# Summing the key exponents of the HGRN levels by two identity products on TensorE

## The chip, the cores and the metric

The kernel runs on one core of one Trainium2 chip. The metric is the device time of one execution, in microseconds (us). The engines have their profile names: PE is TensorE (PEld its weight loads), DVE is VectorE, ACT is ScalarE, POOL is GpSimd and SP is SyncE, which here only issues transfers.

## What is computed

Two layers of a hybrid block over 2048 latent tokens and 256 context tokens, with a model width of 1024. In each layer one input projection feeds four groups of heads: differential attention, a bidirectional gated linear recurrence (HGRN2), windowed attention and an mLSTM. Their outputs are gated, pass one output projection and are added to the stream. The change lies in the recurrence, of which this is the core:

```
cum = jnp.cumsum(log_f, axis=3)
...
diff = cum[:, :, :, :, None, :] - cum[:, :, :, None, :, :]
decay = jnp.exp(jnp.where(tri[:, :, None], diff, -jnp.inf))
a = jnp.einsum('bhnlk,bhnsk,bhnlsk->bhnls', q, k, decay)
o = (jnp.einsum('bhnls,bhnsv->bhnlv', a, v)
     + jnp.einsum('bhnlk,bhnkv->bhnlv', q * jnp.exp(cum), s_start))
```

The matrix `a` needs, for each pair of positions, the product of a query and a key under a decay that depends on both.

## The kernel before

Tokens are worked on in tiles of 128; for HGRN a group is two tiles. Within a tile the kernel builds `a` by halving: at a level m (64, 32, 16, 8, 4, 2, 1) blocks of 2m positions are cut in two halves, and the decay between the halves is split at their border into one factor on the keys and one on the queries. `prepare(li)` makes both factors for a level. The key exponent is a sum of `lk` (log of the key less its cumulated gate) and `cm` (the cumulated gate) at the border; the query exponent is a difference of two places in `cm`. Both lie in the tile `E` (128 partitions, two halves of 512 columns, float32): `E[:, 0]` for keys and `E[:, 1]` for queries. One exponential is taken over both, `QQ` is the query times `E[:, 1]`, and 16 small products (`gA`, 64x64) with the keys give the level's part of `a`, which DVE or ACT puts into `Ad` or `Am`. An eighth step (m = 0, the diagonal) adds whole tiles and is not touched by the change. There are 9 groups in the first layer and 8 in the second, so 17 x 7 = 119 levels.

The HGRN stream runs at the end of each layer, woven together with three others: windowed attention (`ss`, `spv`, with the transposed probabilities `swt`), the mLSTM (`mqk`, `mnum`) and the output stream (`ft` transposes, `fx` the output projection, `xt` the result). Here this is called the woven stretch. `weave` picks the next piece of a stream by due times that are counted in PE time: the helper `mm` (line 94 is its matmul) adds each product's columns, four times as many for float32, to `pe_ns`. `prepare` runs two levels ahead of the products that use it. A scheduler of the language then sets each engine's order from its own model of the times; an engine works through its queue in that order. PSUM tiles of these streams come from `bank`, which hands out four banks in turn under the tag "gp". `lk` and `cm` are loaded from DRAM for each group by the SP queue (line 1463), two buffers deep.

The helpers are one line each, so many operations share a line in the profile: `tt` is line 108, `act` line 105, `mm` line 94 and `tp` line 101.

Of the kernel before, what the change touches and what calls it, by code (L numbers as in the profile page):

```python
# [14 lines left out]
AF = mybir.ActivationFunctionType  # L15
ALU = mybir.AluOpType
# [17 lines left out]
P = 128  # L34
# [25 lines left out]
def view(ap, off, *dims):  # L60

    return bass.AP(ap.tensor, ap.offset + off, [list(ap.ap[0])] + [list(d_) for d_ in dims])
# [11 lines left out]
def kernel(  # L74
# [8 lines left out]
    V, A, G, PE, SP = nc.vector, nc.scalar, nc.gpsimd, nc.tensor, nc.sync  # L83
# [9 lines left out]
    def mm(o, lhsT, rhs, start, stop):  # L93
        PE.matmul(o, lhsT=lhsT, rhs=rhs, start=start, stop=stop)  # L94
        n = 1
        for d_ in rhs.shape[1:]:
            n *= d_
        pe_ns[0] += max(128, n * 4 if rhs.dtype == F32 else n) / 2.4
# [5 lines left out]
    def act(o, i, f, **kw):  # L104
        A.activation(out=o, in_=i, func=f, **kw)  # L105

    def tt(e, o, a, b, op):
        return e.tensor_tensor(out=o, in0=a, in1=b, op=op)  # L108
# [5 lines left out]
    ident = const.tile([P, P], F32, tag="ident", name="ident")  # L114
# [144 lines left out]
    for l in range(n_layers):  # L259
# [941 lines left out]
        with ExitStack() as st4:  # L1201
# [11 lines left out]
            def bank(shape, name):  # L1213
                turn_[0] += 1
                if gps2 and turn_[0] % GPB == 0:
                    return gps2.tile(shape, F32, tag="gp", name=name)
                return gps.tile(shape, F32, tag="gp", name=name, bufs=GPB - 1)
# [226 lines left out]
            def hgrn_stream():  # L1444
# [10 lines left out]
                for g in range(ngrp):  # L1455
# [3 lines left out]
                    def ld(src, tag):  # L1459

                        a = hg.tile([P, 2, 512], F32, tag=tag, name=tag)
                        for d in range(2):
                            SP.dma_start(a[:, d].rearrange("p (b t) -> p b t", b=2),
                                         src[d, :, :, cols].rearrange("b p t -> p b t"))
                        return a
# [4 lines left out]
                    lk, cm = ld(dhk, "lk"), ld(dhc, "cm")  # L1470
# [8 lines left out]
                    def prepare(li):  # L1479

                        m = lv[li]
                        E = hg.tile([P, 2, 512], F32, tag="E", name="E", bufs=EB)
                        if not m:
                            tt(G, E, lk, cm, ALU.add)
                            act(E, E, AF.Exp)
                            tt(G, E[:, 0], E[:, 0], E[:, 1], ALU.add)
                            ops[li] = E[:, 0], q
                            return
                        QQ = hg.tile([P, 512], F32, tag="QQ", name="QQ", bufs=2)


                        n_ = (2 * m, 256 // m)
                        halves = ((m, 2), n_, (1, m))
                        tt(G, view(E[:, 0], 0, *halves), view(lk, 0, (512 + m, 2), n_, (1, m)),
                           view(cm, m - 1, (513, 2), n_, (0, m)), ALU.add)
                        tt(G, view(E[:, 1], 0, *halves), view(cm, 512, (m - 512, 2), n_, (1, m)),
                           view(cm, 512 + m, (-513, 2), n_, (0, m)), ALU.subtract)
                        act(E, E, AF.Exp)
                        tt(V, QQ, q, E[:, 1], ALU.mult)
                        KK = E[:, 0]  # L1500
                        ops[li] = KK, QQ

                    prepare(0)
                    prepare(1)
                    qe = hg.tile([P, 2, 512], F32, tag="qe", name="qe")
                    act(qe, cm, AF.Exp)
                    tt(G, qe, qe, bc(q, 1, 2), ALU.mult)
                    yield 2 * g, HGL, None
                    for li in range(len(lv)):
                        KK, QQ = ops.pop(li)  # L1510
                        pss = [bank([P, 4, 64], "gA") for _ in range(2)]
                        for n in range(4):
                            o = (n % 2) * 256 + n // 2 * P
                            for pa_ in range(2):
                                r_ = slice(pa_ * 64, pa_ * 64 + 64)
                                for a in range(2):
                                    k0, q0 = o + a * 64, o + (a if li else 1 - a) * 64
                                    mm(pss[pa_][a * 64:a * 64 + 64, n], KK[r_, k0:k0 + 64], QQ[r_, q0:q0 + 64],
                                       True, True)
                        for pa_, ps in enumerate(pss):  # L1520
                            if li > 1:
                                V.copy_predicated(Ad[pa_], bc(hgm[:, li], 1, 4), ps)
                            elif li:
                                A.copy(Ad[pa_], ps)
                            else:
                                amv = Am[pa_].rearrange("p i a q -> p (i a) q")
                                for a in range(2):
                                    h_, o_ = slice(a * 64, a * 64 + 64), slice((1 - a) * 64, (1 - a) * 64 + 64)
                                    A.copy(amv[h_, :, o_], ps[h_])
                        if li + 2 < len(lv):  # L1530
                            prepare(li + 2)
                        yield 2 * g + HSTEP * (li + 1), HGW, None
# [201 lines left out]
```

## Time and profile before

| | |
|---|---|
| median of three runs | 4094.21 us (4089.32 to 4104.06) |
| the profiled execution | 4102.18 us, its span 4100.4 us |
| first woven stretch (layer 1) | about 1540 to 2170 us |
| second woven stretch (layer 2) | about 3570 to 4100 us |
| granted TensorE clock, mean | 0.913 of full speed |

Times within the span are counted from its start. The woven stretches are the only places in which the changed lines run; together they are some 1,150 us of the span. In a row of the trace a float32 product shows as two matmul records, and a weight load goes with each; records of one line that follow closely are merged into one row, whose length is that from the first start to the last end.

### The profile page before, as it was taken

The page shows a single profiled execution, that of the slowest core. Times are in us where ns is not written, and L with a number is a line of the kernel's source. Part 1 is how long each engine was busy: PE and PEld are TensorE (multiplying, and loading weights), DVE is VectorE, ACT ScalarE, POOL GpSimd, SP SyncE. Part 2 cuts the span into 40 slices and gives each one's busy share as a digit, 9 for nine tenths or more (in the row PEclk, how much of TensorE's full clock was granted, in tenths as well). Part 3 has the DMA queues.
Part 4 walks back from the last instruction along what each step waited for, and adds up shares of the span by engine and source line. Part 5 has one row for each costly group of instructions (what it writes and reads, how often), then busy time and mean ns, then how long its engine had stood idle before and what let it go on. Part 6 is the DMA issues. An engine that isn't in the chain of part 4 may idle for free. (4 is left out here: it accounts for less than half of the span.)

```text
span 4100.4 us, 77666 instructions
## 1 busy us (share of the span) xinstructions
PE 3358.2 (82%) x29798; PEld 2269.8 (55%) x29798; DVE 2831.4 (69%) x4343; ACT 2330.9 (57%) x4662; POOL 2375.0 (58%) x1701
## 2 busy tenths in 40 slices
PE   6988878888768996888888988778887698758888
PEld 4656645444546765555557466444445476545554
DVE  5158888888896647465544398988888865467665
ACT  4245655556655636566654266656666665456764
POOL 4443455443445538798966535665334564488885
PEclk8999989999989995898889999999998899869999
DMA  6356866667656628577845457667676584366783
GB/s 211 91 149 150 186 136 159 140 141 154 145 128 157 161 95 200 149 194 185 205 119 177 126 125 151 135 140 155 148 162 142 125 193 116 106 162 170 183 194 104
DMA packets 1267259, 622.12 MB, mean 152 GB/s; under 512 B 931972, under 2 KB 1214152, under 8 KB 1266888
## 3 DMA queue, kind: packets, MB, share of 16 engines
q1 hardware_dynamic: 1164520, 490.65, 53.1%
q10 hardware_dynamic: 102368, 126.52, 9.2%
q8 instruction: 234, 3.83, 0.4%
q14 instruction: 137, 1.12, 0.1%
HBM read 291.76 MB, written 131.23 MB: 103 GB/s over the span
## 5 line engine op out<-in xcount | busy, mean ns | idle before, releaser
L108 POOL TENSOR_TENSOR p<-p,p 128x1024 f16<-128x1024 f32 (+2 forms) x264 | 629.4, 2385 | 792.7 <-ACT p L1084 722.8
L105 ACT ACTIVATE p<-scr,sm 128x1024 f32<-128x1024 f32 (+2 forms) x528 | 628.3, 1194 | 417.8 <-DVE sm L1073 145.2
L94 PE MATMUL ptm<-wb,hh 128*128 128x256 f16 (+2 forms) x5024 | 835.6, 273 | 32.6 <-DVE dSs L111 7.9
L1048 DVE TENSOR_REDUCE sm<-scr 128x1 f32<-128x1024 f32 (+2 forms) x528 | 699.3, 1327 | 218.3 <-PE scr L94 214.5
L94 PE MATMUL pfm<-hh,wb 128*128 128x512 f16 (+1 forms) x2592 | 805.7, 375 | 32.7 <-DVE gz L111 10.1
L94 PE MATMUL ptm<-wb,hl 128*128 128x256 f16 (+2 forms) x2512 | 672.1, 273 | 1.7 <-POOL hl L108 1.7
L94 PEld LDWEIGHTS <-wb 128*128 128x128 f16 x3888 | 378.1, 101 | 414.3 <-issue 84.0
L94 PE MATMUL scr<-Ks,Qs 128*128 128x512 f16 (+1 forms) x1296 | 364.8, 381 | 284.5 <-ACT p L105 279.4
L94 PEld LDWEIGHTS <-hh 128*128 128x128 f16 x5024 | 480.1, 100 | 133.9 <-issue 40.0
L94 PE MATMUL pfm<-hl,wb 128*128 128x512 f16 (+1 forms) x1296 | 485.6, 375 | 0.0
L111 DVE SCALAR_TENSOR_TENSOR p<-p,sm,p 128x1024 f32<-128x1024 f32 (+2 forms) x264 | 413.8, 1568 | 8.1
L94 PEld LDWEIGHTS <-Qs 128*128 128x128 f16 x1296 | 130.7, 102 | 425.2 <-issue 354.5
L94 PE MATMUL fx<-wo,mh 128*128 128x512 f16 x1088 | 342.4, 396 | 16.8 <-DVE xt L111 8.5
L1084 ACT CAST p<-p 128x1024 f16<-128x1024 f32 (+2 forms) x264 | 297.7, 1128 | 39.2 <-DVE p L111 33.8
L94 PEld LDWEIGHTS <-wt 128*128 128x128 f16 x4640 | 243.9, 102 | 71.4 <-DMA wt<-p 24.4
L94 PE MATMUL pv<-Vs,wt 128*128 128x128 f16 (+1 forms) x4640 | 258.5, 213 | 21.9 <-DMA wt<-p 13.5
L94 PEld LDWEIGHTS <-hl 128*128 128x128 f16 x2512 | 250.8, 100 | 35.4 <-POOL hl L108 3.4
L108 POOL TENSOR_TENSOR ph<-swp,ph 128x640 f16<-128x640 f32 (+2 forms) x136 | 196.0, 1442 | 53.7 <-ACT ph L1335 44.3
L108 POOL TENSOR_TENSOR E<-lk,cm 128x512 f32<-128x512 f32 (+1 forms) x136 | 204.8, 1506 | 34.6 <-DMA cm<-dhc 17.8
L94 PE MATMUL fx<-wo,mlo 128*128 128x512 f16 x544 | 212.9, 391 | 1.4 <-DVE mlo L108 1.1
L105 ACT ACTIVATE E<-E 128x1024 f32<-128x1024 f32 x136 | 143.2, 1054 | 102.8 <-POOL E L108 98.9
L108 DVE TENSOR_TENSOR QQ<-hq,E 128x512 f32<-128x512 f32 x119 | 143.8, 1214 | 65.2 <-ACT E L105 46.7
(301 smaller groups left out, 6577.2 us busy)
## 6 DMA issues: line engine op xcount, KB each, us to landing
wraw<-in_w_in_dram SPq DMA_DIRECT2D x60, 512.0 KB
dgt<-ga ACTq DMA_DIRECT2D x68, 256.0 KB
r1b<-dr SPq DMA_DIRECT2D x68, 256.0 KB
gtt<-dgt SPq DMA_DIRECT2D x34, 512.0 KB
mraw<-in_w_mod_dram SPq DMA_DIRECT2D x64, 256.0 KB
vi<-dhi SPq DMA_DIRECT2D x49, 256.0 KB
KSb<-dsk SPq DMA_DIRECT2D x56, 192.0 KB
Ks<-dka SPq DMA_DIRECT2D x64, 144.0 KB
```

The costliest lines, as they stand in the source:

```text
L94: PE.matmul(o, lhsT=lhsT, rhs=rhs, start=start, stop=stop)
L105: A.activation(out=o, in_=i, func=f, **kw)
L108: return e.tensor_tensor(out=o, in0=a, in1=b, op=op)
L111: V.scalar_tensor_tensor(out=o, in0=a, scalar=s, in1=b, op0=op0, op1=op1)
L1048: V.tensor_reduce(sm[:, m * 2 + j:m * 2 + j + 1], ps[:, :n], AX.X, ALU.min)
L1084: A.copy(wl[:, :n], p[:, :n])
```

## The change

The sum of the key exponents leaves POOL. A new PSUM tile `e0` (128x512, from `bank`) receives two products with the identity matrix as the stationary operand, the first of `lk`, the second of `cm` accumulated onto it, both read and written through the same strided views as before. ACT takes the exponential from `e0` into `E[:, 0]`, and in a second instruction that of `E[:, 1]`. The difference for the queries stays on POOL.

```diff
-                        tt(G, view(E[:, 0], 0, *halves), view(lk, 0, (512 + m, 2), n_, (1, m)),
-                           view(cm, m - 1, (513, 2), n_, (0, m)), ALU.add)
+                        e0 = bank([P, 512], "e0")
+                        mm(view(e0, 0, *halves), ident, view(lk, 0, (512 + m, 2), n_, (1, m)), True, False)
+                        mm(view(e0, 0, *halves), ident, view(cm, m - 1, (513, 2), n_, (0, m)), False, True)
+                        act(E[:, 0], e0, AF.Exp)
                         tt(G, view(E[:, 1], 0, *halves), view(cm, 512, (m - 512, 2), n_, (1, m)),
                            view(cm, 512 + m, (-513, 2), n_, (0, m)), ALU.subtract)
-                        act(E, E, AF.Exp)
+                        act(E[:, 1], E[:, 1], AF.Exp)
                         tt(V, QQ, q, E[:, 1], ALU.mult)
```

On PE, in the last group of the second layer, near its first levels, the order before has the level's products `gA` between the mLSTM's `mnum` and the output projection's `fx` (`wo` is its weight, `mh` the upper half of the input):

```order
L94 MATMUL mnum<-cst_35559,g0b 128x130
L94 MATMUL mnum<-v_42627,r1b 128x65 x2
L94 MATMUL gA<-QQ,E 64x64 x18
L94 LDWEIGHTS mh
L94 MATMUL fx<-wo_38415,mh 128x512
```

The order after, in the same group, where `e_44350` is the `e0` of its third level:

```order
L94 MATMUL spv<-SVc,swt 128x128
L94 LDWEIGHTS swt
L94 MATMUL spv<-SVc,swt 128x64
L94 MATMUL gA<-QQ,E 64x64 x16
L94 MATMUL e_44350<-lk,ident 128x2x16x16
L94 MATMUL e_44350<-cm,ident 128x2x16x16
L94 MATMUL mnum<-cst_35748,g0b 128x130
L94 MATMUL mnum<-v_43822,r1b 128x65 x2
```

Two products of 512 float32 columns now stand directly behind a level's `gA`, and what follows in PE's queue (`mnum` here) stands behind them.

On POOL, in the same group, the order before has both halves of a level one behind the other:

```order
L108 TENSOR_TENSOR E<-lk,cm 128x2x4x64
L108 TENSOR_TENSOR E<-cm 128x2x4x64
L108 TENSOR_TENSOR E<-lk,cm 128x2x8x32
L108 TENSOR_TENSOR E<-cm 128x2x8x32
L108 TENSOR_TENSOR ph<-swp,ph 128x640
L108 TENSOR_TENSOR yt<-yt,gtt 128x512
```

After, one instruction for each level is left, and the levels stand closer to each other:

```order
L108 TENSOR_TENSOR E<-cm 128x2x16x16
L108 TENSOR_TENSOR yt<-yt,gtt 128x512 x2
L108 TENSOR_TENSOR E<-cm 128x2x32x8
L108 TENSOR_TENSOR ph<-swp,ph 128x640
L108 TENSOR_TENSOR E<-cm 128x2x64x4
```

The first add of a level (`E<-lk,cm`) is gone from POOL's queue at all 119 places; the one for m = 0, over 1024 columns, remains.

## Rows read from the trace of the kernel before

**Rows 1.** The page: busy time, share of the span and instructions of each engine.

```profile
PE 3358.2 (82%) x29798; PEld 2269.8 (55%) x29798; DVE 2831.4 (69%) x4343; ACT 2330.9 (57%) x4662; POOL 2375.0 (58%) x1701
```

**Rows 2.** Stretches: busy time of each engine (x instructions), granted clock, DMA share, GB/s.

```profile
core 0: us, PE busy (x) PEld busy (x) DVE busy (x) ACT busy (x) POOL busy (x), PEclk, DMA share, GB/s
1540.00:1650.00 110.00, 71.32 (x735) 57.27 (x737) 83.11 (x121) 68.89 (x172) 97.72 (x77) 0.58 0.88 201
1650.00:2110.00 460.00, 392.70 (x4129) 270.61 (x4130) 261.89 (x473) 289.65 (x773) 398.21 (x317) 0.87 0.70 176
3570.00:3700.00 130.00, 77.96 (x924) 60.71 (x925) 81.68 (x125) 75.06 (x164) 108.28 (x79) 0.64 0.69 173
3700.00:4040.00 340.00, 294.87 (x3260) 194.69 (x3259) 234.88 (x395) 224.77 (x643) 305.45 (x250) 0.95 0.72 178
```

**Rows 3.** The same stretches, instructions on tile E alone (on DVE: the QQ products).

```profile
1540.00:1650.00 110.00, 14.88 (x356) 12.69 (x360) 15.63 (x11) 12.62 (x12) 32.86 (x25) 0.58 0.88 201
1650.00:2110.00 460.00, 61.62 (x1920) 49.80 (x1920) 63.76 (x52) 63.20 (x60) 160.59 (x120) 0.87 0.70 176
3570.00:3700.00 130.00, 18.00 (x512) 15.04 (x512) 17.68 (x16) 19.00 (x18) 52.08 (x38) 0.64 0.69 173
3700.00:4040.00 340.00, 46.80 (x1486) 35.47 (x1486) 46.73 (x41) 48.38 (x46) 123.70 (x91) 0.95 0.72 178
```

**Rows 4.** The page: chain that ended last, share of the span by engine, by line.

```profile
POOL 4%; PE 3%; DMA 2%; issue 1%; SPq 1%; ACT 1%; DVE 1%; ACTq 0%; POOLq 0%; DVEq 0%
POOL E L108 2%; PE fx L94 1%; POOL yt L108 1%; POOL ph L108 1%; DMA cm<-dhc 1%; PE ptm L94 0%; DMA g0b<-dg 0%; POOL r1b L108 0%; SPq L1385 0%; DMA swt<-ph 0%; PE go L94 0%; DMA gtt<-dgt 0%; POOL g0b L108 0%; SPq L1383 0%; PE gA L94 0%
```

**Rows 5.** Waits in 3575 to 4100: total us, times, longest us.

```profile
ACT E L105 <- POOL E L108: 50.9, 31, 4.5
...
PE spv L94 <- DMA swt<-ph: 29.9, 15, 4.7
...
PE gA L94 <- DVE QQ L108: 17.7, 10, 4.7
POOL E L108 <- DMA cm<-dhc: 14.6, 7, 3.3
```

**Rows 6.** POOL's first adds, 1548 to 2170 and 3575 to 4100: busy us, mean ns | idle before.

```profile
L108 POOL TENSOR_TENSOR E<-lk,cm 128x512 f32<-128x512 f32 x63 | 84.0, 1333 | 18.8 <-DMA cm<-dhc 5.6 <-PE mnum L94 5.5 <-PE gA L94 4.6
...
L108 POOL TENSOR_TENSOR E<-lk,cm 128x512 f32<-128x512 f32 x56 | 77.6, 1387 | 15.8 <-DMA cm<-dhc 12.3 <-DMA lk<-dhk 2.1 <-PE gA L94 1.4
```

**Rows 7.** PE in order of time: start us, length us, operation, records.

```profile
3741.94 0.39 PE L94 MATMUL mnum<-cst,g0b 128*128 128x130 f32 x2
3742.16 0.56 PE L94 MATMUL mnum<-v,r1b 128*128 128x65 f32 x4
...
3770.67 0.69 PE L94 MATMUL gA<-QQ,E 64*64 64x64 f32 x32
3771.29 0.60 PE L94 MATMUL fx<-wo,mh 128*128 128x512 f16 x2
3771.74 0.38 PE L94 MATMUL fx<-wo,mlo 128*128 128x512 f16 x1
```

**Rows 8.** A dense stretch of the input projections (columns as in rows 2).

```profile
1400.00:1450.00 50.00, 47.54 (x391) 34.92 (x390) 24.14 (x49) 24.18 (x47) 23.36 (x20) 1.00 0.46 125
```

**Rows 9.** ACT by shape: the exponential of E, one of 512 columns, reads of PSUM.

```profile
L105 ACT ACTIVATE E<-E 128x1024 f32<-128x1024 f32 x136 | 143.2, 1054 | 102.8 <-POOL E L108 98.9
...
L105 ACT ACTIVATE ga<-ga 128x512 f32<-128x512 f32 x68 | 42.6, 626 | 4.9 <-DVE carry L650 3.2 <-POOL fm L108 0.6
...
L105 ACT ACTIVATE swp<-ss,ssm 128x512 f32<-128x512 f32 x16 | 10.9, 678 | 21.3 <-DVE ssm L1331 18.2 <-DMA v<-dmv 3.0
...
L1550 ACT COPY O<-go 128x512 f32<-128x512 f32 x17 | 9.7, 572 | 0.5 <-PE go L94 0.5
```

**Rows 10.** The chain where a group begins: start us, us, what.

```profile
3912.60 0.47 SPq L1463
3913.11 5.27 DMA cm<-dhc
3918.45 0.18 issue
3918.65 0.19 issue
3918.84 4.20 POOL E L108 x4
```

## The prediction

> **What bounds the kernel now.** I read the page first: over the whole span PE is busy 82%, DVE 69%, POOL 58% [rows 1]. That is an average over stages, and the change touches one stage only, so the second view is that of stretches. Each woven stretch has a start-up and a steady part [rows 2]. In the steady parts (1650 to 2110 and 3700 to 4040, together 800 us) PE is busy 392.7 of 460 and 294.9 of 340 us, 85% and 87%; POOL is busy 398.2 and 305.5 us, 87% and 90%. Two engines are nearly full at once. PE stands idle 67.3 + 45.1 = 112 us there, and its clock is granted at 0.87 and 0.95 of full speed. In the start-ups (110 and 130 us) the clock is 0.58 and 0.64, near the lower of its two levels, 1.2 and 2.4 GHz; PE is busy 71.3 and 78.0 us and POOL 97.7 and 108.3 us, so POOL leads there, with DMA at a share of 0.88 in the first.
>
> The chain that ended last runs more through POOL than through any other engine (4%), and E is POOL's largest line on it, 2% [rows 4]. The waits agree: ACT's exponential waits 50.9 us for POOL's E in the second woven stretch, and PE waits 17.7 us for QQ, which follows from it [rows 5]. So there is a reason to take work from POOL. The question is what it costs where it goes, because PE is as full as POOL.
>
> **What is removed.** 119 adds on POOL, 63 of 84.0 us and 56 of 77.6 us together, 161.6 us or 1.36 us each [rows 6]. In a group of seven levels that is 9.5 us of POOL.
>
> **What is added on PE.** Two float32 products of 512 columns for each level. The trace has no such product, so I take the nearest float32 one: `mnum` of 130 columns starts at 3741.94 and the next line at 3742.16, so 0.22 us or 1.69 ns a column [rows 7]. Two `fx` of 512 half-precision columns start at 3771.29 and the next one at 3771.74, 0.22 us each, a fourth per column [rows 7]. A product of 512 float32 columns is then 512 x 1.69 ns = 0.87 us, a level 1.73 us, and 119 levels 206 us at the full clock. At the lower level of the clock it is twice that. For size: all 16 `gA` products of a level take 0.62 us (3770.67 to 3771.29) [rows 7], so PE's work for a level becomes almost four times what it was.
>
> **Where it falls.** The QQ products count the levels in each stretch: 11 and 52, 16 and 41 (one too many in all, at a border) [rows 3]. For the steady parts that is 52 x 1.73 = 90.0 us and 41 x 1.73 = 70.9 us at the full clock.
> - At the clock granted now: 392.7 + 90.0 / 0.87 = 496.1 us and 294.9 + 70.9 / 0.95 = 369.5 us, 865.6 us of PE in 800 us. Without any idle time that is 66 us more. The densest stretch that I found, in the input projections, has PE busy 47.54 of 50 us, 95.1% [rows 8]. With that share, 865.6 / 0.951 = 910 us: +110.
> - With the clock at 1.00, as it is in that dense stretch: 392.7 x 0.87 + 90.0 = 431.6 and 294.9 x 0.95 + 70.9 = 351.0, together 782.6, / 0.951 = 823 us: +23.
>
> The clock should rise, since it is lowest in the start-ups, where PE is idle most, and 1.00 in the dense stretch [rows 2, 8]; but it will not be full throughout, as PE still waits for other engines. I take the middle of 23 and 110: **+67 us**. The Trainium skill, "TensorE: Matmul & The Clock Gate", Part 1 on the clock gate, says that the throttled state is the default and that activity releases it. By that rule alone the second case would hold, +23. The trace agrees in its direction: 0.58 and 0.64 in the start-ups, 0.87 and 0.95 behind them.
>
> **Start-ups.** 11 and 16 levels cost 11 x 1.73 / 0.58 = 32.8 and 16 x 1.73 / 0.64 = 43.3 us of PE, 76 in all, and PE is idle for 38.7 and 52.0 us [rows 2, 3]. POOL, which leads there, is relieved by 27 x 1.36 = 37 us. The bounds are -37 and +76; I take 0, since the two act against each other and DMA is nearly full anyway. The cover is PE's idle time; where it doesn't fit, up to 76 us come back.
>
> **The transfer of cm.** A group begins with a load of lk and cm. In the row shown cm is issued last at 3913.11 and takes 5.27 us, with POOL starting E at 3918.84 [rows 10]. POOL waited 14.6 us for cm in the second woven stretch and 5.6 in the first [rows 5, 6], 20 in all. After the change PE waits too: the first `e0` of a group stands in its queue, and behind it stand `fx`, `ss` and `spv` of other streams. The bounds are 0 and 17 x 5.3 = 90 us. I take half of the waits that POOL has, **+10**, since PE will mostly be late itself.
>
> **ACT, bank and DVE.** One exponential of 1054 ns becomes two: 626 ns from SBUF, and from PSUM between 572 (a copy) and 678 (an exponential with a sum), so 144 to 250 ns more, 17 to 30 us over 119 levels [rows 9]. ACT is busy 63% and 66% in the steady parts [rows 2], so I count nothing; without that cover it is 30. `e0` holds one of the four banks from its first product to the end of its exponential, while a level's `gA` takes two; the trace has no row for a wait that this makes, and its bounds are with the second rival. DVE's work is the same.
>
> **Sum.** 67 + 0 + 10 = +77 us on the profiled execution's 4102.2, so 4179; the median of the runs shown is 8.0 lower, so **4171 us**. The forecast's own range is 4117 (+23, no other cost) to 4224 (+110 and the 20 us of waits for cm).
>
> **Rivals.**
> 1. *POOL sets the pace and PE has room (faster).* For it: POOL's place on the chain [rows 4] and ACT's 50.9 us of waiting [rows 5]. The gain would be the first adds' part of E on the chain: E is 2%, 82 us; all of POOL's work on E in rows 3 is 369 us, the first adds are 161.6 or 44% of it, so 36 us less: 4058. It decides if PE can take 161 to 178 us more into 112 us of idle time; even with the clock at 1.00 PE would have to be 98% busy (782.6 of 800). Against it: no stretch that I saw is so dense. Chance 0.10.
> 2. *The products do not fill idle time (much slower).* They stand behind the level's `gA`, so they wait with it, for QQ, for a bank, for cm, as `spv` does for swt (29.9 us) [rows 5], and everything else in PE's queue waits with them. Then nothing is hidden: 206 us, or the 865.6 us of above at the present 86% busy, 1007 us in place of 800. That gives 4300, with cm 4310. Chance 0.15.
> 3. *No measurable change.* The clock rises to 1.00 and the products fit with 2% idle: 800 us again, 4094. A change of 0.3%, 12 us, is about the least that a measurement of this kernel tells from none. Chance 0.06.
> 4. *Strided products are slow.* The views step through `lk`, `cm` and PSUM in pieces of m columns. If a strided product took twice the time, 206 us more would come on top: near 4377; if only m = 1 did, 17 levels x 1.73 = 29 us: 4200. No row shows a strided float32 product. The Trainium skill, "PSUM — Partial Sum Buffer", Specifications, says that any access pattern that is not contiguous slows matmuls significantly, which speaks against the change; no run so far shows it. A float32 column already takes four times a half-precision one [rows 7], which leaves time for each write. Chance 0.05.
>
> The forecast itself has 0.64. Slower is 0.64 + 0.15 + 0.05 = 0.84, the same 0.06, faster 0.10. The range 4085 to 4310 leaves out most of the first rival (0.09), half of the second (0.07) and most of the fourth (0.03).
>
> **What the changed profile would show.** `e0` rows on PE, four records a level, 1.7 us from the first start to the next line; PE busy above 92% in the steady parts and POOL below 75%; a higher granted clock; the waits of ACT for POOL's E much smaller, and in their place waits for PE. The time between the output stream's tiles grows. If `e0` rows take over 2.5 us at the full clock, rival 4 is right; if PE's idle share stays at 14% while the stretches lengthen by 200 us, rival 2; if POOL is still the fuller engine, rival 1. The prediction is wrong if the products are far cheaper than 0.87 us, or if the new order moves other streams' work apart so that a wait which I haven't seen grows.

## The result, and the profile after

The changed kernel takes 4161.05 us (median; 4157.16 to 4166.45), the kernel before in the same comparison 4094.26 us. The ratio is 1.0161, 95% interval 1.0139 to 1.0183: 67 us slower, where 77 were forecast. The profiled execution has a span of 4155.3 us against 4100.4, 55 us more: 12 less than the medians, since the one of the kernel before took 4102.18 us, more than its median, and that of the changed kernel 4157.16, less than its median.

The page's first part, against [rows 1]:

```profile
PE 3494.7 (84%) x30274; PEld 2297.4 (55%) x30274; DVE 2808.8 (68%) x4343; ACT 2336.3 (56%) x4781; POOL 2205.8 (53%) x1582
```

PE gained 476 records (four for each of 119 levels) and 136.5 us of busy time, POOL lost 119 instructions and 169 us, ACT gained 119 instructions and 5.4 us.

The stretches of the changed kernel, columns as in [rows 2]; the second steady part is cut at 4020 us here, so that experiments can be set beside it:

```profile
1540.00:1650.00 110.00, 82.93 (x799) 56.16 (x799) 75.09 (x121) 69.89 (x184) 79.67 (x63) 0.80 0.85 195
1650.00:2110.00 460.00, 438.91 (x4299) 272.13 (x4299) 257.55 (x468) 290.19 (x822) 324.88 (x262) 0.98 0.69 175
3700.00:4020.00 320.00, 294.72 (x2746) 182.87 (x2745) 171.21 (x317) 188.67 (x561) 204.85 (x174) 0.95 0.65 162
```

The same cut of the kernel before:

```profile
3700.00:4020.00 320.00, 279.94 (x3070) 184.75 (x3072) 217.70 (x366) 213.34 (x612) 285.60 (x234) 0.95 0.73 179
```

In the steady parts PE is now busy 95% and 92%, POOL 71% and 64%: one full engine in place of two. In the first the clock went from 0.87 to 0.98; in the second it was 0.95 and stayed there. The counts show what that means for the work done: in 460 us of the first steady part PE made 4299 matmul records, the products among them, against 4129 before; in 320 us of the second 2746 against 3070. By this the loss sits in the second.

The output stream says the same. First the kernel before, then the changed one: instructions on the tile `xt`, count, durations in ns, first and last start in us (the 18 POOL adds belong to the first layer's tiles, the 32 DVE sums to the second's).

```profile
L111 DVE SCALAR_TENSOR_TENSOR xt<-fx,xt x32: 676/682/694, 3676.4 to 4092.8; 128x512 f32<-128x512 f32 x32
L108 POOL TENSOR_TENSOR xt<-xt,yt x18: 2337/2357/2798, 1670.6 to 2161.1; 128x1024 f32<-128x1024 f32 x18
```

```profile
L111 DVE SCALAR_TENSOR_TENSOR xt<-fx,xt x32: 677/692/693, 3684.0 to 4147.4; 128x512 f32<-128x512 f32 x32
L108 POOL TENSOR_TENSOR xt<-xt,yt x18: 2337/2354/2394, 1661.5 to 2159.7; 128x1024 f32<-128x1024 f32 x18
```

From its first tile to its last the output stream takes 498.2 us in place of 490.5 in the first layer (+8) and 463.4 in place of 416.4 in the second (+47). The first tile comes 9 us earlier (1670.6 to 1661.5), and from the end of the first layer's stream to the first tile of the second's it is 9 us longer (1515.3 to 1524.3). Only the 47 stands clear of the scatter between traces: in E4 and E7 below, which have all the work of the kernel before and no product, the first tile comes at 1682.7 and 1661.0 us, the first layer's stream takes 474.7 and 503.3 us, and the second's 408.2 and 413.2.

The products themselves, in the changed kernel's PE rows in order of time, as in [rows 7]:

```profile
1662.10 1.02 PE L94 MATMUL e<-lk,ident 128*128 128x512 f32 x2
1662.96 1.02 PE L94 MATMUL e<-cm,ident 128*128 128x512 f32 x2
1663.82 0.33 PE L94 MATMUL go<-vi,Am 128*128 128x64 f32 x2
...
3785.86 1.17 PE L94 MATMUL e<-lk,ident 128*128 128x512 f32 x2
3786.86 1.06 PE L94 MATMUL e<-cm,ident 128*128 128x512 f32 x2
```

A level takes 1.72 us from 1662.10 to the next line at 1663.82; this is m = 64. At 3785.86, a level of m = 2, the first product alone takes 1.00 us to the second's start. The last level of the group that begins at 1662.10, m = 1, takes 1.89 us:

```profile
1693.66 1.15 PE L94 MATMUL e<-lk,ident 128*128 128x512 f32 x2
1694.65 1.06 PE L94 MATMUL e<-cm,ident 128*128 128x512 f32 x2
1695.55 0.25 PE L94 MATMUL spv<-SVb,swt 128*128 128x128 f16 x2
```

The view of the tile `e`, for the changed kernel, tells what else belongs to it (min/median/max in ns; then PE's pauses for lk and ACT's waits for the products, us and times):

```profile
L94 PE MATMUL e<-lk,ident x238: 592/612/1222, 1542.4 to 4085.5; 128*128 128x512 f32 x119
L94 PE MATMUL e<-cm,ident x238: 592/592/1061, 1547.4 to 4086.4; 128*128 128x512 f32 x119
L105 ACT ACTIVATE E<-e x119: 569/597/617, 1552.0 to 4087.1; 128x512 f32<-128x512 f32 x119
...
  DMA lk<-dhk: 4.7, 2
...
  ACT E L105: 61.0, 39
```

ACT waits 61.0 us for the products. The waits of 3575 to 4100 us answer to [rows 5] (the changed kernel's stream is not quite at its end there):

```profile
ACT E L105 <- POOL E L108: 50.1, 28, 6.8
ACT E L105 <- PE e L94: 30.4, 19, 5.7
...
POOL E L108 <- DMA cm<-dhc: 15.8, 5, 4.3
...
PE gA L94 <- ACT E L105: 13.1, 6, 3.2
...
PE spv L94 <- DMA swt<-ph: 8.0, 6, 2.2
...
PE gA L94 <- DVE QQ L108: 4.5, 2, 4.2
```

ACT waits for POOL as long as before, now for the difference that is left there, and for PE besides. PE's wait for swt has shrunk from 29.9 to 8.0 us; that of `gA` for QQ and E together is 17.6, where it was 17.7 for QQ alone. PE paused once for a transfer before work on `e`: the 4.7 us above are one pause, counted on the weight load (2.4 us) and on the product (2.2 us).

### The profile page after: what moved, and what is told of

It reads as the page before. It is cut to its first block, busy times and chain, and to the rows that moved or that the text cites. A ratio compares the mean times of both kernels' runs of the same rounds, so it can differ in the third digit from the quotient of the medians.

```text
span 4155.3 us, 78592 instructions
## 1 busy us (share of the span) xinstructions
PE 3494.7 (84%) x30274; PEld 2297.4 (55%) x30274; DVE 2808.8 (68%) x4343; ACT 2336.3 (56%) x4781; POOL 2205.8 (53%) x1582
## 5 line engine op out<-in xcount | busy, mean ns | idle before, releaser
L108 POOL TENSOR_TENSOR ph<-swp,ph 128x640 f16<-128x640 f32 (+2 forms) x136 | 186.2, 1369 | 119.5 <-ACT ph L1335 99.6
L108 POOL TENSOR_TENSOR E<-cm 128x512 f32<-128x512 f32 x119 | 147.7, 1245 | 62.7 <-DMA cm<-dhc 37.9
L94 PEld LDWEIGHTS <-mh 128*128 128x128 f16 x1088 | 103.3, 103 | 121.0 <-issue 40.6
```

## The experiments

Each kernel was compared with the kernel before in the same session; that one's medians were 4094.74 (E1 to E4), 4100.31 (E5 to E8) and 4094.41 us (E9 to E11). Differences are taken within a session, but for those between the changed kernel (beside 4094.26) and E1, E2 or E5.

**E1 to E4: which part costs, and which order.**

E1 takes both the add and the products away:

```diff
-                        e0 = bank([P, 512], "e0")
-                        mm(view(e0, 0, *halves), ident, view(lk, 0, (512 + m, 2), n_, (1, m)), True, False)
-                        mm(view(e0, 0, *halves), ident, view(cm, m - 1, (513, 2), n_, (0, m)), False, True)
-                        act(E[:, 0], e0, AF.Exp)
+                        act(view(E[:, 0], 0, *halves), view(lk, 0, (512 + m, 2), n_, (1, m)), AF.Exp, scale=1e-3)
```

> Neither the add on POOL nor the products on PE: ACT takes the exponential of the strided lk alone (scaled by 0.001, to stay finite), so the border's term is left out and the decays are not the reference's; instruction counts elsewhere are those of the changed kernel. Theory (the changed kernel is paced by PE, and its 67 us are the products' streaming time less what the clock gives back): without the products the time falls below the kernel before, 4050 to 4090 us, as POOL's first adds are gone and PE has its old idle time. Rival (order and waits that the new weave brings, not the products): it stays above 4130 us. Rival (POOL never paced anything): 4094 within 8 us.

It took 4045.42 us, ratio 0.9888 (0.9867 to 0.9910): 49 us faster than before, just below the range expected. So the first adds did hold the kernel back, and the loss comes with the products and their PSUM tile. E1 takes away two things at once, POOL's work and the wait of the key exponential for a sum; E8 below, which keeps the sum but moves part of it off POOL, gains 27 us, so POOL's work is at least a good part of it. Its row for the first steady part:

```profile
1650.00:2110.00 460.00, 405.65 (x4351) 270.41 (x4352) 270.80 (x507) 309.65 (x889) 343.64 (x277) 0.96 0.74 187
```

The clock is 0.96 here without any of the new products; before, it was 0.87 [rows 2].

E2 pays for both: the changed kernel with POOL's add kept, ahead of the products.

```diff
+                        tt(G, view(E[:, 0], 0, *halves), view(lk, 0, (512 + m, 2), n_, (1, m)),
+                           view(cm, m - 1, (513, 2), n_, (0, m)), ALU.add)
                         e0 = bank([P, 512], "e0")
```

> The changed kernel with the first add kept on POOL too (its result is overwritten by the exponential from PSUM). Theory (PE paces, POOL's relief is worth little once the products stand on PE): 4161 to 4185 us. Rival (POOL still paces, and the relief hides most of a much larger cost on PE): the 162 us of POOL come back, well over 4200 us.

It took 4186.43 us, ratio 1.0236 (1.0209 to 1.0263), 25 us more than the changed kernel and just above the range expected. With E1 this closes a square of four kernels. The products cost 92 us where the adds stay (4186.4 against 4094.7) and 116 us where they are gone (4161.0 against 4045.4). The relief of POOL is worth 49 us without the products and 25 us with them. The loss of 67 us is what is left of a cost of 116 us after a gain of 49. In the trace of E2 the first steady part, with the adds on POOL and the products on PE, is this:

```profile
1650.00:2110.00 460.00, 424.24 (x4153) 261.84 (x4154) 263.21 (x444) 282.29 (x796) 377.39 (x304) 0.98 0.68 170
```

E3 makes the products in the first layer alone.

```diff
+                        if l == 0:
                             e0 = bank([P, 512], "e0")
...
+                        else:
+                            tt(G, view(E[:, 0], 0, *halves), view(lk, 0, (512 + m, 2), n_, (1, m)),
+                               view(cm, m - 1, (513, 2), n_, (0, m)), ALU.add)
```

> The products in the first layer alone, the adds on POOL in the second. Theory (in the first woven stretch the granted clock had room to rise, from 0.87 to 0.98, and the products live on that; in the second it had none): 4085 to 4100 us, and so some 60 us for the second layer alone. Rival (each level costs the same in both layers): 63 of 119 levels, half of the 67 us, near 4130 us.

4106.06 us, ratio 1.0024 (1.0010 to 1.0038), 11 us slower: above the range expected, and far from the rival's 4130. In the first layer the change costs little on balance, but not nothing.

E4 is the kernel before with the weave's clock advanced as if the products were there.

```diff
                            view(cm, m - 1, (513, 2), n_, (0, m)), ALU.add)
+                        pe_ns[0] += 2 * 512 * 4 / 2.4
```

> The kernel before, with the weave's PE time advanced by two products for each level although none is made: the streams are woven as in the changed kernel, with the work of the kernel before. Theory (the products themselves cost): 4085 to 4110 us. Rival (the new order of the streams costs): 4130 us or more.

4093.53 us, ratio 1.0001 (0.9987 to 1.0015). The due times that the products shift cost nothing by themselves. The order that the scheduler makes of real products is not tested by this.

**E5 to E7: size, layer, ACT.**

E5 makes one product for each level:

```diff
-                        mm(view(e0, 0, *halves), ident, view(lk, 0, (512 + m, 2), n_, (1, m)), True, False)
-                        mm(view(e0, 0, *halves), ident, view(cm, m - 1, (513, 2), n_, (0, m)), False, True)
-                        act(E[:, 0], e0, AF.Exp)
+                        mm(view(e0, 0, *halves), ident, view(lk, 0, (512 + m, 2), n_, (1, m)), True, True)
+                        act(E[:, 0], e0, AF.Exp, scale=1e-3)
```

> The changed kernel with one product for each level in place of two: that of cm at the border is left out (and the exponent scaled by 0.001), so the decays are not the reference's. Theory (the products cost by their streaming time on PE: 116 us for two, between the changed kernel's 4161 and the 4045 of the run without products): half, 4095 to 4110 us. Rival (what costs is that e0 takes a bank and that ACT waits for it, whatever it streams): above 4135 us.

4114.35 us, ratio 1.0036 (1.0024 to 1.0048), 4 us above the range. Without products a kernel is 49 us below the kernel before (E1), with one 14 above, with two 67 above. So the first costs 63 us and the second 53: most goes with the number of products, and some 10 us may go with `e0` itself (its bank, ACT's wait), which these runs do not separate from the scatter between sessions.

E6 makes the products in the second layer alone.

```diff
-                        if l == 0:
+                        if l == 1:
```

> The products in the second layer alone. Theory (the second woven stretch had its clock at 0.95 already, so most of the loss is there): the rest of the 67 us that the first layer alone doesn't show, 4140 to 4160 us. Rival (the two layers' losses overlap or depend on each other): below 4130 us.

4156.71 us, ratio 1.0131 (1.0115 to 1.0148), 56 us slower. With E3's 11 that is 68, the whole of the 67: the layers add up, and five sixths are in the second.

E7 is the kernel before with the exponential in two instructions:

```diff
-                        act(E, E, AF.Exp)
+                        act(E[:, 0], E[:, 0], AF.Exp)
+                        act(E[:, 1], E[:, 1], AF.Exp)
```

> The kernel before with the exponential of E in two instructions of 512 columns, all else as it was. Theory (ACT has room; two short exponentials cost it 24 us of busy time in all): 4088 to 4108 us. Rival (the second exponential in ACT's queue delays QQ and with it PE's gA): 4120 us or more.

4097.46 us, ratio 0.9985 (0.9967 to 1.0004). No change that can be told from none.

**E8, E9, E11: the relief without PE; E10: the weave once more.**

E8 moves the first add of levels 1, 3 and 5 of each group to DVE, with no product:

```diff
-                        tt(G, view(E[:, 0], 0, *halves), view(lk, 0, (512 + m, 2), n_, (1, m)),
+                        tt(V if li % 2 else G, view(E[:, 0], 0, *halves), view(lk, 0, (512 + m, 2), n_, (1, m)),
```

> The kernel before with the first add of the levels 1, 3 and 5 of each group on DVE in place of POOL (51 of 119), no product on PE. Theory (the relief of POOL is worth up to 49 us where the add costs nothing elsewhere, and DVE is busy 57 to 69 percent in the steady parts): 4065 to 4090 us. Rival (DVE and POOL hold each other up, or QQ comes later behind the adds): 4094 us or more.

4073.60 us, ratio 0.9928 (0.9912 to 0.9945): faster than both kernels. DVE's busy time in the first steady part rises from 261.89 us [rows 2] to 296.51, POOL's falls from 398.21 to 377.31:

```profile
1650.00:2110.00 460.00, 409.27 (x4238) 278.91 (x4227) 296.51 (x514) 299.46 (x827) 377.31 (x302) 0.91 0.70 181
```

E9 moves all seven.

```diff
-                        tt(G, view(E[:, 0], 0, *halves), view(lk, 0, (512 + m, 2), n_, (1, m)),
+                        tt(V, view(E[:, 0], 0, *halves), view(lk, 0, (512 + m, 2), n_, (1, m)),
```

> The kernel before with all 119 first adds on DVE, no product on PE. Theory (the relief of POOL is worth up to 49 us, and DVE takes on some 1.2 us a level, twice what the half did): 4050 to 4080 us, not much better than the half, since DVE comes to about 84 percent in the second steady part. Rival (DVE becomes the pace, or the shared path of DVE and POOL does): above 4090 us.

4121.31 us, ratio 1.0061 (1.0043 to 1.0079): a miss, on the rival's side. In the first woven stretch of E8, the adds on DVE take 1008 ns each:

```profile
L108 DVE TENSOR_TENSOR E<-lk,cm 128x512 f32<-128x512 f32 x26 | 26.2, 1008 | 10.4 <-DMA cm<-dhc 9.8 <-DMA v<-dmv 0.6
```

and in E9 1309 ns:

```profile
L108 DVE TENSOR_TENSOR E<-lk,cm 128x512 f32<-128x512 f32 x62 | 80.5, 1309 | 12.7 <-DMA cm<-dhc 11.0 <-issue 1.0 <-PE gA L94 0.8
```

but that is some 19 us in this stretch (62 x 0.3), and DVE's busy share in E9 is no more than this, in the first and the second steady part:

```profile
1650.00:2110.00 460.00, 394.30 (x4236) 262.25 (x4235) 330.06 (x539) 291.80 (x786) 349.81 (x267) 0.92 0.72 179
3700.00:4020.00 320.00, 276.89 (x2841) 184.20 (x2842) 235.88 (x381) 198.05 (x554) 226.00 (x184) 0.89 0.72 172
```

72% of 460 and 74% of 320 us, so the expectation's reason (DVE nearly full, 84%) does not hold, and no engine is fuller than PE with 86% and 87%. The loss lies in the second layer (the table below): the granted clock there is 0.89, where it was 0.95 before. That the adds delay what queues behind them on DVE, QQ and the maxima of the windowed attention among it, would fit, but it was only argued; why three adds on DVE gain 27 us and seven lose 27 stays open.

E11 moves four, of levels 1, 2, 4 and 5.

```diff
-                        tt(G, view(E[:, 0], 0, *halves), view(lk, 0, (512 + m, 2), n_, (1, m)),
+                        tt(V if li % 3 else G, view(E[:, 0], 0, *halves), view(lk, 0, (512 + m, 2), n_, (1, m)),
```

> The kernel before with the first add of levels 1, 2, 4 and 5 on DVE (68 of 119), the others on POOL, no product on PE. Theory: between the half and the whole, 4055 to 4080 us. Rival (the gain of the half was in its order, not in the relief): no better than 4085 us.

4072.07 us, ratio 0.9947 (0.9927 to 0.9967), in the range expected and as E8 within the intervals.

E10 is the changed kernel with the products left out of the weave's count.

```diff
                         act(E[:, 0], e0, AF.Exp)
+                        pe_ns[0] -= 2 * 512 * 4 / 2.4
```

> The changed kernel with the products left out of the weave's PE time, so that the streams are woven as in the kernel before. Theory (the products cost by streaming, the order hardly matters): 4145 to 4185 us. Rival (part of the 67 us is the new weave): below 4130 us.

4162.36 us, ratio 1.0165 (1.0145 to 1.0185), the changed kernel's time. The count plays no part, as in E4.

**The same runs by layer.** The output stream cuts each trace in two: the start of the first layer's last tile (the last POOL add on `xt`), and the time from there to the start of the last sum of the second layer's (DVE). In the traces of E1 and E2:

```profile
L111 DVE SCALAR_TENSOR_TENSOR xt<-fx,xt x32: 668/682/692, 3614.1 to 4032.1; 128x512 f32<-128x512 f32 x32
L108 POOL TENSOR_TENSOR xt<-xt,yt x18: 2337/2357/2807, 1660.8 to 2116.1; 128x1024 f32<-128x1024 f32 x18
```

```profile
L111 DVE SCALAR_TENSOR_TENSOR xt<-fx,xt x32: 675/684/693, 3707.7 to 4173.0; 128x512 f32<-128x512 f32 x32
L108 POOL TENSOR_TENSOR xt<-xt,yt x18: 2337/2357/2392, 1673.1 to 2182.4; 128x1024 f32<-128x1024 f32 x18
```

The same for all that bear on it, one trace each, in us:

| kernel | first layer's last tile | from there to the second's last |
|---|---|---|
| adds on POOL, no product: before, E4, E7 | 2161.1, 2157.4, 2164.3 | 1931.7, 1920.6, 1924.6 |
| neither: E1 | 2116.1 | 1916.0 |
| both: E2 | 2182.4 | 1990.6 |
| products, no add: changed, E10 | 2159.7, 2174.3 | 1987.7, 1977.8 |
| products in the first layer alone: E3 | 2176.5 | 1920.2 |
| products in the second layer alone: E6 | 2155.9 | 1984.5 |
| adds partly on DVE: E8, E11 | 2129.8, 2129.6 | 1929.4, 1934.9 |
| adds all on DVE: E9 | 2151.2 | 1960.3 |

In the first layer the relief of POOL is worth 40 to 48 us (E1), the products cost 18 to 27 where the adds stay (E2) and 44 to 60 where they are gone. In the second the relief is worth 4 to 16 us, and the products cost 59 to 70 with the adds and 62 to 72 without. So the first layer's small loss doesn't mean that its products are free: they use up a gain that only this layer has. POOL was 87% busy in the first steady part and 90% in the second [rows 2], and its relief paid almost only in the first.

## Why the prediction was right, point by point

**What bounds the kernel.** Two engines nearly full, POOL and PE, was the right reading on the whole: E1 shows POOL's part (49 us to be had), E2 PE's (92 us for the products alone). By layer it holds for POOL in the first alone; in the second POOL was busy 90%, and its relief was worth 4 to 16 us.

**The price of a level.** 1.73 us from a product of 130 columns; 1.72 measured at m = 64, 1.89 in the row of m = 1 above. The median over all levels, from the first start to the next line, is 1.82 us, 5% more than forecast.

**The steady parts.** +67 was forecast from PE's occupancy between two clocks, at 95.1% busy. E3 and E6 measure 11 and 56 us for the two layers, with PE at 95% and 92% in the changed kernel. Taken by layer, the forecast's two sums are -6 and +62 us for the first steady part, +29 and +49 for the second: the first came out near the lower end, the second beyond the upper one. In the first steady part the clock rose from 0.87 to 0.98, and the relief of POOL set time free (40 to 48 us in E1), which the products filled. In the second the clock was 0.95 before and 0.95 after, the relief gave 4 to 16 us, PE reached 92% and not 95.1%, and most of the products went into the time. The step that did not hold is "the middle of 23 and 110", a mean over two layers that behave differently. That the total came out near it is luck. The mechanism, PE filled by the products and POOL relieved, is what the runs show.

**Why the clock rose.** The forecast tied it to PE's fuller work. In the first steady part two runs raise it, each by one half of the change: E1, with no products and PE busy 88%, shows 0.96, and E2, with the adds still on POOL and PE busy 92%, shows 0.98. Both, and the changed kernel, have a busier PE there (405.65, 424.24 and 438.91 us) than the kernel before (392.70). But the traces of E4 and E7, with all the adds and no product, show 0.92 and 0.87 with PE busy 390.79 and 393.98 us, so some 0.05 is scatter, and busy time alone does not settle it. The Trainium skill, "TensorE: Matmul & The Clock Gate", Part 1 (activity releases the throttle), is not contradicted by E1 and E2. By that rule alone the forecast was +23, and 67 were measured. In the second steady part PE is busier too (294.72 against 279.94 us of 320) and the clock stays at 0.95; what holds it there no run shows.

**Start-ups: 0.** The first tile came 9 us earlier, and what lies between the two streams of output tiles, the second start-up in it, is 9 us longer. Right in sum, but kernels with the same work differ by more than that in the first (1661.0 us in E7, 1682.7 in E4), so it is not shown to the microsecond.

**The transfer of cm: +10.** Too much: PE paused once for a transfer before work on `e`, 2.2 us for lk. As the forecast's own sentence had it, PE mostly comes late itself.

**The waits.** ACT's waits for POOL's E should have become much smaller; they are 50.1 us against 50.9 in the second layer. The difference for the queries still comes from POOL, and ACT waits for that.

**ACT and DVE: nothing.** Right: E7 is 0.9985 with an interval that holds 1. The exponential from PSUM takes 597 ns and that of E's other half 629, 172 more than the 1054 of the one before, or 20 us over 119 levels, within the 17 to 30 of the forecast. ACT's busy time in all grew by 5 us only; what it did less elsewhere was not looked into.

**The rivals.** POOL sets the pace and PE has room: half true. The relief was worth more than the 36 us of its estimate (49, E1), but PE had not the room for the products. The products fill no idle time: refuted, 92 to 116 us were paid of the 206 of streaming that were forecast. No measurable change: refuted, PE did not become 98% busy and the clock stayed at 0.95 in the second layer. Strided products are slow: refuted as it was put, twice the time. The second products (of cm) have a median of 592 ns a record in pieces of 64 to 4 columns and 610 in pieces of 2 and 1, 3% more. The first ones (of lk) go from a median of 592 ns at m = 64 to 716 at m = 2 and 613 at m = 1, and it is not shown whether the stride or what stands before them does it. What the Trainium skill says in "PSUM — Partial Sum Buffer", Specifications, that accesses which are not contiguous slow matmuls significantly, is seen here as these 3%, and at most as the 21% of the first products at m = 2.

**The signs.** Those of PE above 92% and POOL below 75% in the steady parts, of 1.7 us a level and of longer times between output tiles came (the last in the second layer). The granted clock rose in one layer alone, and ACT's waits for POOL did not fall.

## What to carry to other kernels

Before work moves from one full engine to another, take the occupancy of both in each stage, and price the moved work on its new engine: an add of 1.36 us on POOL became 1.72 to 1.9 us on PE, which was as full. What a relief is worth and what the new place costs can be had apart with two kernels, one that leaves the work out and one that does it twice; here 49 us of gain stood against 92 to 116 of cost. Moving three or four of the seven adds to DVE, which was less busy, gave 0.993 and 0.995 of the time before.

Busy shares do not tell alone which engine sets the pace: POOL was 90% busy in the second layer, and taking its adds away was worth 4 to 16 us there against 40 to 48 in the first. A mean over stages hides that, and so does a small loss in one stage, which can be a large cost that eats a gain. Cut each trace at a fixed piece of work and compare the four kernels on either side. And take the scatter from traces of kernels with the same work, before a difference of 10 us or of 0.05 in the granted clock is read as an effect.

## What the runs showed of the hardware that was not expected

A product of 512 float32 columns with the identity takes two records, each of 592 ns at the median, whether its operand and its output lie in pieces of 64 or of 4 columns, and with a step of zero in the moving operand; in pieces of 2 and of 1 it is 610 ns (the products of cm). The exponential of 512 columns took 597 ns from PSUM and 629 from SBUF, medians of 119 each, so PSUM is the cheaper source for ACT here. And the granted clock of TensorE in the first steady part rose with no product added on PE: it was 0.87 to 0.92 in four kernels with that layer's adds on POOL and no products in it (before, E4, E6, E7) and 0.96 in E1, where POOL was busy 343.64 us in place of 398.21. One trace each shows it.
